# Banks for the last chunk's norm transposes, the first pair's first split, and later splits of the second matrix's tiles, in a fused decoder layer

## The chip, the cores and the metric

The kernel runs on one core of a Trainium2 chip. The metric is the device time of one execution in microseconds (us). The core has five engines that run at the same time, each through its own list of instructions in order: PE (TensorE, matrix products and transposes), DVE (VectorE), ACT (ScalarE), POOL (GpSimd) and SP (SyncE, which here only issues transfers). They wait for each other through semaphores. PE writes its results to PSUM, a small memory of banks; DVE or ACT must read a bank before PE may start something new in it.

## The reference

One layer of a decoder for a prompt of 1024 tokens and 8 sample tokens (1032 tokens together), width 1024, feed-forward width 2816, all in fp32:

```
h = x * (1 + scale1) + shift1
[q,k,v | rq,rk,rv,rg | ga,gb] = h @ w_in
A = dilated sliding-window attention @ w_att_out ;  B = retention @ w_ret_out
x = LN1(alpha * x + gate1 * ((sigmoid(ga) * A + sigmoid(gb) * B) @ w_o))
x = LN2(alpha * x + gate2 * SwiGLU(x * (1 + scale2) + shift2))
```

What follows is about three steps of it: the product with `w_o`, the first layer norm (LN1), and the feed-forward part, whose first matrix `w_ffn_in` holds a gate half g and an up half u, and whose second matrix is `w_ffn_out`.

## The kernel before

**Products.** Every fp32 operand is split into a high and a low part (hi and lo) that PE takes in its fp32r type, and each product is three matmuls: hi by hi, hi by lo, lo by hi. A split is a cast on ACT (hi) and a subtraction on DVE or POOL (lo). Weights come as tiles of 128 x 8 x 128 from the pool `stream` with three buffers each for raw, hi and lo. PSUM banks have four tags: d (three banks), a (two), b (two), o (one). Larger SBUF tiles come from `slots`, a queue of free buffers: whoever takes a buffer that was used before waits for its last readers.

**Order.** Up to the output projection a scheduler of the language may move instructions. From there on `pe`, `dve`, `act`, `pool` and `sp` are wrappers (class `InOrder`, whose call is line 116), which keep the order in which the code is written. That is why most rows below show line 116; they are told apart by the names of their tiles.

**Output projection.** Lines 1168 on run over four chunks of tokens, `for ci in (3, 2, 1, 0)`, and in each over eight weight tiles f = 0 to 7. `wo_cols(f)` issues the load of tile f on SP's queue (line 944) and splits it: even tiles on DVE, odd ones on POOL. PE then makes 24 matmuls into a bank d, and ACT empties the bank into one of four tiles `gm` (line 1180), two weight tiles to each. After every tile `step_pending()` advances the norms of the chunks before by one step.

**Norms.** `norm_chunk` makes two blocks of 128 tokens for a chunk; `norm_block` first transposes the eight parts of `gm` into two banks a, four in each, adds the residual into x on DVE, takes mean and variance (`bn`, `bnmv`), the square root on ACT (`bnr`, line 593) and scales x. Its second half transposes x into two banks b, from which `h2` (the input of the feed-forward part) is scaled and shifted. For the last chunk (ci = 0, the branch `fixed`) the instructions are in written order, and ACT does the scaling and all of `h2`. The blocks of this chunk are stepped within the first pairs of the feed-forward part.

**First matrix in pairs.** A pair i takes 128 columns of g and of u and makes both for half of the tokens in seven products instead of eight, with sums of weights and of tokens (a scheme of Winograd's kind). `pair_load(q)` loads g and u (512 KB each) on SP's queue; `pair_sums(q)` forms four sums of weights on POOL (`w_s`, `w_s4`, and u in place); `pair_split(q, j)` splits the four weight tiles, j = 0 to 3; `combine` sums and splits the tokens into X1 to X7. `pair_steps` holds the products: two accumulations go on in a bank b and a bank a over several products, and each is copied out on ACT or summed on DVE into c11, c12, c21, c22 before the next product is added to it. These names show in the rows as `c`. There are 26 jobs q: 0 to 3 with token half 1 alone, 4 to 21 with both halves, 22 to 25 with half 0 alone. Results go to DRAM as `ffd`.

**Second matrix.** While jobs 22 to 25 run, the results of half 1 come back: `ff_load` brings a tile (`ffr`, 260 KB) on SP's queue and `ff_split` splits it into `xk`, one after each step s_ from job 22 on. `out_load(G)` loads the weights of group G of the second matrix; in job 25 at steps 0, 1 and 2 for groups 0, 1 and 2, and their splits stand at steps 3 and 5 and after the loop. Behind the loop stand the loads and splits of `xk` that are left, and then the groups of products, three to each 128 output columns, whose result rows y pass through LN2.

Of the kernel before, what the change touches and what calls it, by code (L numbers as in the profile page):

```python
# [121 lines left out]
def tile_hybrid_decoder_step(ctx: ExitStack, tc: tile.TileContext, a, o):  # L122
    nc = tc.nc
# [27 lines left out]
    def abank(shape=(128, 512)):  # L151
        return bank("a", shape, 2)

    def bbank(shape=(128, 512)):
        return bank("b", shape, 2)
# [14 lines left out]
    def split(raw, hi, lo, eng=nc.vector):  # L170
        nc.scalar.copy(hi, raw)  # L171
        eng.tensor_sub(lo, raw, hi.bitcast(F32))  # L172
# [108 lines left out]
    pb = bbank((128, 48))  # L281
# [657 lines left out]
        act.copy(hi, raw)  # L939
        dve.tensor_sub(lo, raw, hi.bitcast(F32))  # L940

    def wo_cols(f):
        raw = stream.tile([128, 8, 128], F32, tag="raw", name="w_raw")
        dma_w.dma_start(raw[:], a["w_o"][:, 128 * f:128 * f + 128].rearrange("(k p) c -> p k c", p=128))
        hi = stream.tile([128, 8, 128], F32R, tag="hi", name="w_hi")
        lo = stream.tile([128, 8, 128], F32R, tag="lo", name="w_lo")
        split(raw[:], hi[:], lo[:], nc.gpsimd if f % 2 else nc.vector)
        return hi, lo

    def norm_block(tb, rows, gm, t0, h2):  # L950
        fixed = t0 == 0
        V, A = (dve, act) if fixed else (nc.vector, nc.scalar)
        x = slots.alloc((128, D), name="x1")
        dma_o.dma_start(x[:rows], a["x_prompt"][tb:tb + rows] if tb < S else a["x_sample"])
        for half in range(2):
            pz = abank((rows, 512))
            for j in range(4):
                f = 4 * half + j
                pe.transpose(pz[:, 128 * j:128 * j + 128],
                             gm[f // 2][:, f % 2, tb - t0:tb - t0 + rows], ident[:])  # L960
            c = slice(512 * half, 512 * half + 512)
            V.scalar_tensor_tensor(x[:rows, c], x[:rows, c], ALPHA, pz, op0=OP.mult, op1=OP.add)
        st = late.tile([128, 2, 6], F32, tag="bn", name="bn", bufs=2)
        for i in range(2):
            V.bn_stats(st[:rows, i, :], x[:rows, 512 * i:512 * i + 512])
        mv, r = ln_aggr(st, rows, V, A)
        if fixed:
            nb = late.tile([128, 1], F32, tag="nb", name="nb", bufs=2)
            V.tensor_scalar(nb[:rows], mv[:rows, 0:1], r[:rows], -1.0, op0=OP.mult, op1=OP.mult)
            A.activation(x[:rows], x[:rows], AF.Identity, scale=r[:rows], bias=nb[:rows])  # L970
        else:
            V.tensor_scalar(x[:rows], x[:rows], mv[:rows, 0:1], r[:rows], op0=OP.subtract, op1=OP.mult)
        dma_o.dma_start(xr[tb:tb + rows], x[:rows])
        yield
        for half in range(2):
            pb = bbank((128, 4, rows))
            for j in range(4):
                f = 4 * half + j
                pe.transpose(pb[:, j, :], x[:rows, 128 * f:128 * f + 128], ident[:rows, :rows])
            c4 = slice(4 * half, 4 * half + 4)  # L980
            if tb < S:
                for j in range(4):
                    f = 4 * half + j
                    if half or fixed:
                        A.activation(h2[:, f, :], pb[:, j, :], AF.Identity, bias=B2[:, f, 8:9],
                                             scale=G2[:, f, 8:9])
                    else:
                        V.tensor_scalar(h2[:, f, :], pb[:, j, :], G2[:, f, 8:9], B2[:, f, 8:9],
                                                op0=OP.mult, op1=OP.add)
            else:  # L990
                nc.vector.tensor_mul(h2[:, c4, :], pb, G2[:, c4, 0:NB])
                nc.vector.tensor_add(h2[:, c4, :], h2[:, c4, :], B2[:, c4, 0:NB])
        slots.free(x)
        yield
# [71 lines left out]
    def pair_sums(q):  # L1066
        if q >= NJ:
            return
        g, _, u, _ = raws[q]
        s_, e = slots.alloc((128, 8, 128), name="w_s"), slots.alloc((128, 4, 128), name="w_s4")  # L1070
        pool.tensor_add(s_[:, 4:8, :], u[:, 0:4, :], u[:, 4:8, :])
        pool.tensor_sub(s_[:, 0:4, :], s_[:, 4:8, :], g[:, 0:4, :])
        pool.tensor_sub(e[:], g[:, 4:8, :], s_[:, 0:4, :])
        pool.tensor_sub(u[:, 0:4, :], g[:, 0:4, :], u[:, 0:4, :])
        raws[q] = [g, s_, u, e]

    def pair_split(q, j):
        if q >= NJ:
            return
        raw = raws[q][j]  # L1080
        if j < 3:
            hi, lo = [stream.tile([128, 8, 128], F32R, tag=n, name="w_" + n)[:] for n in ("hi", "lo")]
        else:
            t = slots.alloc((128, 8, 128), F32R, name="w4")
            ring[q] = t
            hi, lo = t[:, 0:4, :], t[:, 4:8, :]
        psplit(raw[:], hi, lo)
        if j:
            slots.free(raw)
        if rolling[0]:  # L1090
            roll(hi)
        ring[q, j] = (hi, lo)
# [74 lines left out]
    for ci in (3, 2, 1, 0):  # L1167
        t0, n = QCH[ci]
        gm = [slots.alloc((128, 2, 264), name="gm") for _ in range(4)]
        for f in range(8):  # L1170
            ps = dbank((128, n))
            o0 = t0 % 512
            whi, wlo = wo_cols(f)
            for k, m in enumerate(mix):
                xhi, xlo = m[ci // 2][:, 0, o0:o0 + n], m[ci // 2][:, 1, o0:o0 + n]
                pe.matmul(ps, whi[:, k, :], xhi, start=k == 0, stop=False)
                pe.matmul(ps, whi[:, k, :], xlo, start=False, stop=False)
                pe.matmul(ps, wlo[:, k, :], xhi, start=False, stop=k == 7)
            dst = gm[f // 2][:, f % 2, :]
            nc.scalar.activation(dst[:, :256], ps[:, :256], AF.Copy, scale=modT[:, GATE1 + f, 8:9])  # L1180
            if n > 256:
                nc.vector.tensor_mul(dst[:, 256:n], ps[:, 256:n], modT[:, GATE1 + f, 0:NB])
            step_pending()
            if ci == 0 and f == 4:
                pair_load(0)
            if ci == 0 and f == 6:
                pair_sums(0)
        if ci % 2 == 0:
            slots.free(*[m[ci // 2] for m in mix])
        pending.append(after_chunk(ci, gm))  # L1190
        if ci == 0:
            pair_load(1)
            pair_split(0, 0)
            pair_split(0, 1)

    xk = [{}, {}]
# [18 lines left out]
    def out_load(G):  # L1215
        if G >= NG:
            return
        _, f, o0, nk = GROUPS[G]
        raw = graw[G] = stream.tile([128, nk, 128], F32, tag="raw", name="w_raw")
        ks = ORDER[o0:o0 + nk]  # L1220
        k1 = next((j for j in range(1, nk) if ks[j] != ks[j - 1] + 1), nk)
        for j0, j1 in ((0, k1), (k1, nk)):
            if j1 > j0:
                sp.dma_start(raw[:, j0:j1, :], w_fo[128 * ks[j0]:128 * (ks[j0] + j1 - j0), 128 * f:128 * f + 128]
                             .rearrange("(k p) c -> p k c", p=128))
# [14 lines left out]
    for q, (i, halves) in enumerate(JOBS):  # L1240
        rolling[0] = len(halves) == 2
        if q == FFC:
            free_x({1: [t for p in X[1].values() for t in p]})
        steps = [pair_steps(q, i, half) for half in halves]
        for s_ in range(7):
            for _ in range(2):
                for g_ in steps:
                    next(g_)
            if s_ == 0:
                pair_split(q, 2)  # L1250
                pair_sums(q + 1)
            elif s_ == 1:
                pair_split(q, 3)
                pair_load(q + 2)
            elif s_ == 2:
                pair_split(q + 1, 0)
            elif s_ == 4:
                pair_split(q + 1, 1)
            if q < LEAD and s_ % 2 == 0:
                step_pending()  # L1260
            if q >= FFC:
                if waiting:
                    ff_split(waiting.popleft())
                for _ in range(1 if len(slots.free_list) >= 6 and kq < FFC else 0):
                    waiting.append(ff_load(1, ORDER[kq]))
                    kq += 1
            if q == NJ - 1:
                if s_ in (0, 1, 2):
                    out_load(s_)
                if s_ in (3, 5):  # L1270
                    out_split(s_ // 2 - 1)
        slots.free(ring[q])
# [204 lines left out]
```

## Time and profile before

| | |
|---|---|
| runs | 1928.22, 1928.94, 1923.56 us; median 1928.22 |
| profiled execution | 1921.71 us, of which the span shown is 1919.9 |
| mean granted clock of PE in it | 0.983 of full speed |
| PE busy | 1826.7 us, 95% of the span |
| weight loads on PE (beside the matmuls) | 1736.6 us, 90% |
| DVE, ACT, POOL busy | 979.9 (51%), 680.9 (35%), 365.0 (19%) |
| moved by DMA | 256.39 MB |

The profiled execution is one run of the kernel with the hardware profiler; all rows come from it. A busy share is a mean over the whole span, so it doesn't tell where an engine waits. The views used below do: busy time by stretch, what an engine waited for in a stretch, the list of one engine's instructions in order of time with the idle time ahead of each and what ended it, and the chain of work followed back from the end. Names are those of the tiles in the code, `out<-in`; a digit behind a name is left out in them, so X1 to X7 are X, h2 is h and c4 is c.

### The profile page before, as it was taken

How to read it: one execution, taken by the hardware profiler on the slowest of the kernel's cores; microseconds unless marked ns; L12 is line 12 of the kernel's file. 1: busy time of each engine (PE TensorE's matmuls, PEld its weight loads, DVE VectorE, ACT ScalarE, POOL GpSimd, SP SyncE). 2: the span in 40 equal slices, each digit the busy share in tenths (PEclk: the TensorE clock that was granted, in tenths of full speed). 3: DMA queues.
4: the chain of work that ended last, by engine and by line, in shares of the span. 5: the costliest groups of instructions: out<-in, count | busy, mean ns of one | idle time of the engine just before them, and what ended most of it. 6: DMA issues, size and time to landing. Idle time of an engine off the chain costs nothing.

```text
span 1919.9 us, 33798 instructions
## 1 busy us (share of the span) xinstructions
PE 1826.7 (95%) x13974; PEld 1736.6 (90%) x13974; DVE 979.9 (51%) x2020; ACT 680.9 (35%) x1338; POOL 365.0 (19%) x435
## 2 busy tenths in 40 slices
PE   7999999999999999999999976999999997999997
PEld 5979889889899998999999965999999997999997
DVE  4733636686534432211555956555455457534844
ACT  3252332443434342122424645333333335223321
POOL 2000010330100000000004345444444343100000
PEclk9999999999999999999999988999999998899999
DMA  9312131681321344431116552356777535525631
GB/s 283 94 37 95 35 104 34 159 289 45 103 67 58 95 151 135 152 112 53 56 53 188 189 175 77 124 162 196 247 241 253 205 91 181 177 88 160 195 120 64
DMA packets 271627, 256.39 MB, mean 134 GB/s; under 512 B 9749, under 2 KB 251261, under 8 KB 270706
## 3 DMA queue, kind: packets, MB, share of 16 engines
q1 hardware_dynamic: 251170, 149.02, 26.8%
q0 software_dynamic: 20176, 105.12, 15.9%
q8 instruction: 109, 1.79, 0.4%
q14 instruction: 44, 0.36, 0.1%
q10 hardware_dynamic: 128, 0.10, 0.0%
HBM read 223.30 MB, written 74.94 MB: 155 GB/s over the span
## 4 chain that ended last, share of the span: by engine, by line
PE 69%; issue 14%; DVE 5%; DMA 5%; POOL 3%; ACT 3%; SPq 1%; DVEq 0%; POOLq 0%; ACTq 0%
PE ps_d L116 10%; PE ps_b L116 10%; PE ps_d L208 9%; PE ps_d L210 9%; PE ps_d L209 9%; PE ps_a L116 5%; PE ps_d L376 2%; PE ps_d L374 2%; PE ps_d L375 2%; POOL w_s L116 2%; PE ps_a L490 1%; PE ps_b L508 1%; PE ps_o L517 1%; DMA vb<-dv 1%; PE ps_a L241 1%
## 5 line engine op out<-in xcount | busy, mean ns | idle before, releaser
L208 PE MATMUL ps_d<-h_hi,w_hi 128*128 128x384 f32 (+1 forms) x1008 | 325.3, 323 | 0.0
L210 PE MATMUL ps_d<-h_hi,w_lo 128*128 128x384 f32 (+1 forms) x1008 | 323.5, 321 | 0.0
L209 PE MATMUL ps_d<-h_lo,w_hi 128*128 128x384 f32 (+1 forms) x1008 | 323.1, 321 | 0.0
L172 DVE TENSOR_TENSOR w_lo<-w_raw,w_hi 128x1024 fp32r<-128x1024 f32 x88 | 103.8, 1179 | 255.3 <-ACT w_hi L171 254.7
L116 PE MATMUL ps_b<-X,w_hi 128*128 128x260 f32 (+1 forms) x1056 | 199.5, 289 | 22.0 <-ACT c L116 20.5
L116 DVE TENSOR_TENSOR w_lo<-w_raw,w_hi 128x1024 fp32r<-128x1024 f32 (+1 forms) x100 | 132.8, 1330 | 163.8 <-ACT w_hi L116 163.7
L171 ACT CAST w_hi<-w_raw 128x1024 fp32r<-128x1024 f32 x104 | 103.9, 999 | 259.2 <-PE ps_d L209 200.1
L208 PEld LDWEIGHTS ps_d<-h_hi,w_hi 128*128 128x128 f32 x1008 | 189.3, 188 | 5.2 <-DVE A L859 3.3
L210 PEld LDWEIGHTS ps_d<-h_hi,w_lo 128*128 128x128 f32 x1008 | 189.5, 188 | 1.7 <-issue 1.2
L209 PEld LDWEIGHTS ps_d<-h_lo,w_hi 128*128 128x128 f32 x1008 | 189.5, 188 | 0.8 <-issue 0.4
L116 PEld LDWEIGHTS ps_b<-X,w_hi 128*128 128x128 f32 x1056 | 167.5, 194 | 23.8 <-ACT c L116 22.1
L116 PE MATMUL ps_b<-X,w_lo 128*128 128x260 f32 (+1 forms) x528 | 152.0, 288 | 0.8 <-DVE w_lo L116 0.8
L116 ACT CAST w_hi<-w_raw 128x1024 fp32r<-128x1024 f32 (+1 forms) x100 | 101.2, 1014 | 107.4 <-PE ps_b L116 91.6
L116 PE MATMUL ps_d<-X,w_hi 128*128 128x260 f32 (+1 forms) x704 | 132.8, 289 | 0.0
L116 PE MATMUL ps_d<-xk,w_hi 128*128 128x260 f32 (+1 forms) x704 | 130.3, 285 | 0.0
L376 PE MATMUL ps_d<-w_lo,h_hi 128*128 128x256 f32 x448 | 127.3, 285 | 0.7 <-DVE w_lo L172 0.7
L116 PE MATMUL ps_b<-xk,w_hi 128*128 128x260 f32 (+1 forms) x704 | 127.7, 282 | 0.0
L374 PE MATMUL ps_d<-w_hi,h_hi 128*128 128x256 f32 x448 | 127.5, 285 | 0.0
L375 PE MATMUL ps_d<-w_hi,h_lo 128*128 128x256 f32 x448 | 126.7, 283 | 0.0
L116 PEld LDWEIGHTS ps_d<-X,w_hi 128*128 128x128 f32 x704 | 112.2, 195 | 0.0
L116 PEld LDWEIGHTS ps_d<-xk,w_hi 128*128 128x128 f32 x704 | 109.6, 191 | 0.1
L116 PEld LDWEIGHTS ps_b<-xk,w_hi 128*128 128x128 f32 x704 | 108.3, 189 | 0.0
(363 smaller groups left out, 4168.9 us busy)
## 6 DMA issues: line engine op xcount, KB each, us to landing
w_raw<-w_in SPq DMA_DIRECT2D x56, 512.0 KB, 4.4
w_raw<-w_ffn_in SPq DMA_DIRECT2D x52, 512.0 KB, 5.0
ada_raw<-w_ada SPq DMA_DIRECT2D x32, 512.0 KB, 4.8
w_raw<-w_o SPq DMA_DIRECT2D x32, 512.0 KB, 4.5
w_raw<-w_ffn_out SPq DMA_DIRECT2D x32, 512.0 KB, 3.7
sample_k<-cache_k POOLq DMA_DIRECT2D x8, 2047.0 KB, 8.8
sample_v<-cache_v POOLq DMA_DIRECT2D x8, 2047.0 KB, 9.4
ada_raw<-w_ada SPq DMA_DIRECT2D x32, 256.0 KB, 5.1
```

The lines of the kernel that those rows point to most:

```text
L116: return self.tc.keep_in_program_order(f(*args, **kw))
L171: nc.scalar.copy(hi, raw)
L172: eng.tensor_sub(lo, raw, hi.bitcast(F32))
L208: nc.tensor.matmul(ps, whi[:, k0 + k, :], xhi[:, t0:t0 + n], start=f, stop=False)
L209: nc.tensor.matmul(ps, whi[:, k0 + k, :], xlo[:, t0:t0 + n], start=False, stop=False)
L210: nc.tensor.matmul(ps, wlo[:, k0 + k, :], xhi[:, t0:t0 + n], start=False, stop=l)
L241: nc.tensor.matmul(ps[32 * g:32 * g + 32], cs[:, k0 + k, :], w[:, k], start=k0 + k < 4, stop=k0 + k >= 4)
L374: nc.tensor.matmul(ps[:, j, :], xh, whi, start=k == 0, stop=False)
L375: nc.tensor.matmul(ps[:, j, :], xl, whi, start=False, stop=False)
L376: nc.tensor.matmul(ps[:, j, :], xh, wlo, start=False, stop=k == 7)
L490: nc.tensor.matmul(sb[hh][:, p, :nk], qT[p][r, 128 * bi:128 * bi + 128], kT[p][r, k0:k0 + nk], start=True, stop=True)
L508: nc.tensor.transpose(pb[:, j, :], pm[h][:, 128 * b:128 * b + 128], ident[:])
```

## The change

It has three parts.

- The norm transposes of the last chunk (`fixed`) no longer go through the banks a and b, which the pairs use for accumulations that stay open over several products. Their first half goes to bank o, the second to a bank d.
- The weights of pair 0 are asked for behind tile 6's load (after f = 5) and no longer behind tile 5's (after f = 4). The sums of pair 0 and the split of its first tile stand ahead of the evacuation of tile 7, and no longer after tile 6 and after the loop. Tile 7 is split on DVE instead of POOL.
- In jobs 22 to 25 `ff_split` is called only while more than two loaded tiles are waiting, so splits come later, and more of them are left for after the loop. The weights of groups 0 and 1 of the second matrix are asked for in job 24, at steps 3 and 5, and those of group 2 in job 25 at step 2.

```
-    def wo_cols(f):
+    def wo_cols(f, eng):
...
-        split(raw[:], hi[:], lo[:], nc.gpsimd if f % 2 else nc.vector)
+        split(raw[:], hi[:], lo[:], eng)
...
-            pz = abank((rows, 512))
+            pz = (abank if not fixed else dbank if half else obank)((rows, 512))
...
-            pb = bbank((128, 4, rows))
+            pb = (bbank if not fixed else dbank if half else obank)((128, 4, rows))
...
-            whi, wlo = wo_cols(f)
+            whi, wlo = wo_cols(f, nc.gpsimd if f % 2 and (ci or f < 7) else nc.vector)
...
+            if ci == 0 and f == 7:
+                pair_sums(0)
+                pair_split(0, 0)
             nc.scalar.activation(dst[:, :256], ps[:, :256], AF.Copy, scale=modT[:, GATE1 + f, 8:9])
...
             step_pending()
-            if ci == 0 and f == 4:
+            if ci == 0 and f == 5:
                 pair_load(0)
-            if ci == 0 and f == 6:
-                pair_sums(0)
...
         if ci == 0:
             pair_load(1)
-            pair_split(0, 0)
             pair_split(0, 1)
...
             if q >= FFC:
-                if waiting:
+                if len(waiting) > 2:
                     ff_split(waiting.popleft())
...
+            if q == NJ - 2 and s_ in (3, 5):
+                out_load(s_ // 2 - 1)
             if q == NJ - 1:
-                if s_ in (0, 1, 2):
-                    out_load(s_)
+                if s_ == 2:
+                    out_load(2)
```

How this moves instructions shows best in the lists of the built kernels. SP's queue around the loads of pair 0 (`w_ffn_in`; `w_o` are the tiles of the output projection, the last three of 32 being tiles 5, 6 and 7 of the last chunk), before:

```order
L944 DMA w_raw<-w_o 128x8x128 x29
L116 DMA w_raw<-w_ffn_in 128x8x128
L116 DMA w_raw_328_11522<-w_ffn_in 128x8x128
L944 DMA w_raw<-w_o 128x8x128 x3
L116 DMA w_raw<-w_ffn_in 128x8x128
L116 DMA w_raw_331_11628<-w_ffn_in 128x8x128
```

and after:

```order
L944 DMA w_raw<-w_o 128x8x128 x30
L116 DMA w_raw<-w_ffn_in 128x8x128
L116 DMA w_raw_328_11554<-w_ffn_in 128x8x128
L944 DMA w_raw<-w_o 128x8x128 x2
L116 DMA w_raw<-w_ffn_in 128x8x128
L116 DMA w_raw_331_11632<-w_ffn_in 128x8x128
```

Tile 5's load has passed the two loads of pair 0, which stand ahead of tile 6's now.

ACT at the end of the output projection (`gm_11273` takes tiles 4 and 5, `gm_11274` tiles 6 and 7; the casts of line 116 are the pair's), before:

```order
L171 CAST w_hi<-w_raw 128x1024
L985 ACTIVATE h_326_11364<-ps_b,B_10198,G_10197 128x128 x4
L171 CAST w_hi<-w_raw 128x1024
L1180 ACTIVATE gm_11273<-ps_d,modT 128x256 x2
L1180 ACTIVATE gm_11274<-ps_d,modT 128x256 x2
L116 CAST w_hi<-w_raw 128x1024
L116 CAST w_hi<-w_s_11589 128x1024
L116 COPY c_332_11639<-ps_b 128x260
```

and after, where the evacuation's line is 1183:

```order
L171 CAST w_hi<-w_raw 128x1024
L985 ACTIVATE h_326_11364<-ps_b,B_10198,G_10197 128x128 x4
L171 CAST w_hi<-w_raw 128x1024
L1183 ACTIVATE gm_11273<-ps_d,modT 128x256
L116 CAST w_hi<-w_raw 128x1024
L1183 ACTIVATE gm_11273<-ps_d,modT 128x256
L1183 ACTIVATE gm_11274<-ps_d,modT 128x256 x2
L116 CAST w_hi<-w_s_11620 128x1024
L116 COPY c_332_11639<-ps_b 128x260
```

The first cast of pair 0 has moved ahead of the evacuations of tiles 5, 6 and 7; the cast of its sum `w_s` has stayed behind them.

PE where the first block of the last chunk is transposed, between the first and the second product of pair 0, before:

```order
L116 MATMUL ps_b<-X_306_11107,w_lo 128x260
L116 MATMUL ps_a<-ident,gm_11271 128x128 x2
L116 MATMUL ps_a<-ident,gm_11272 128x128 x2
L116 MATMUL ps_a<-ident,gm_11273 128x128 x2
L116 MATMUL ps_a<-ident,gm_11274 128x128 x2
L116 MATMUL ps_d<-X_308_11109,w_hi 128x260
```

and after:

```order
L116 MATMUL ps_b<-X_306_11107,w_lo 128x260
L116 MATMUL ps_o<-ident,gm_11271 128x128 x2
L116 MATMUL ps_o<-ident,gm_11272 128x128 x2
L116 MATMUL ps_d<-ident,gm_11273 128x128 x2
L116 MATMUL ps_d<-ident,gm_11274 128x128 x2
L116 MATMUL ps_d<-X_308_11109,w_hi 128x260
```

The place among PE's instructions is the same; the banks differ.

DVE in job 22 (`xk` are the splits of the second matrix's tiles, `w_lo` and `w_483` those of the pair's weights, `c` its sums), before:

```order
L116 TENSOR_TENSOR c_478_16521<-c_478_16521,ps_d 128x256
L116 TENSOR_TENSOR w_483_16564<-w_s_475_16329,w_483_16564 128x512
L116 TENSOR_TENSOR xk_16548<-ffr_16546,xk_16548 128x520
L116 TENSOR_TENSOR w_lo<-w_raw,w_hi 128x1024
L116 TENSOR_TENSOR xk_16575<-ffr_16573,xk_16575 128x520
L116 TENSOR_TENSOR xk_16597<-ffr_16595,xk_16597 128x520
L116 TENSOR_TENSOR c_478_16521<-c_478_16521,ps_a 128x256
```

and after:

```order
L116 TENSOR_TENSOR c_478_16521<-c_478_16521,ps_d 128x256
L116 TENSOR_TENSOR w_483_16564<-w_s_475_16329,w_483_16564 128x512
L116 TENSOR_TENSOR w_lo<-w_raw,w_hi 128x1024
L116 TENSOR_TENSOR xk_16548<-ffr_16546,xk_16548 128x520
L116 TENSOR_TENSOR c_478_16521<-c_478_16521,ps_a 128x256
```

Three splits of `xk` stood ahead of the sum with bank a (c22); one is left there. Of the 22 tiles of half 1, 15 instead of 19 are split within jobs 22 to 25, and seven instead of three behind the loop.

## Rows read from the trace of the kernel before

**Rows 1.** Busy time by stretch: length, PE, PEld, DVE, ACT, POOL, PEclk, DMA share, GB/s.
```profile
1100.00:1150.00 50.00, 36.32 (x275) 35.49 (x275) 26.48 (x41) 22.55 (x37) 23.41 (x17) 0.90 0.59 180
1150.00:1200.00 50.00, 31.50 (x207) 30.61 (x207) 33.39 (x40) 26.45 (x51) 25.71 (x19) 0.81 0.24 74
1600.00:1650.00 50.00, 41.70 (x297) 41.09 (x298) 31.75 (x44) 22.80 (x40) 13.09 (x16) 0.86 0.55 160
```

**Rows 2.** PE's waits, 1020 to 1220: waited for, us in total, times, longest.
```profile
PE ps_b L116 <- ACT h L116: 10.6, 2, 8.2
PE ps_b L116 <- ACT c L116: 8.6, 3, 4.8
PE ps_a L116 <- DVE x L116: 6.8, 1, 6.8
PE ps_b L116 <- DVE x L972: 4.6, 1, 4.6
...
PE ps_b L116 <- ACT w_hi L116: 1.5, 1, 1.5
...
PE ps_b L116 <- DVE w_lo L116: 0.8, 1, 0.8
```

**Rows 3.** PE's waits, 1500 to 1700.
```profile
PE ps_b L116 <- ACT c L116: 11.8, 5, 3.9
PE ps_d L116 <- DVE w_lo L116: 4.5, 1, 4.5
PE ps_a L116 <- DVE c L116: 2.3, 1, 2.3
```

**Rows 4.** The chain that ended last, 1095 to 1215: start, us, what.
```profile
1108.07 6.03 DMA w_raw<-w_o
...
1197.64 2.97 PE ps_b L116 x12
...
1202.27 1.45 PE ps_a L116 x12
```

**Rows 5.** SP's queue near 1103: start, us, line, operation, out<-in.
```profile
1103.65 0.99 SPq L116 DMA_DIRECT2D w_raw<-w_ffn_in  x2
```

**Rows 6.** ACT in order of time: start, us, operation, idle time before and what ended it.
```profile
1114.20 1.04 ACT L171 CAST w_hi<-w_raw 128x1024 fp32r<-128x1024 f32 x1 [6.30 <-DMA w_raw<-w_o]
1115.15 0.29 ACT L593 ACTIVATE bnr<-bnmv,eps 128x1 f32<-128x1 f32 x1
...
1132.87 1.04 ACT L116 CAST w_hi<-w_raw 128x1024 fp32r<-128x1024 f32 x1
...
1154.43 0.38 ACT L116 COPY c<-ps_b 128x260 f32<-128x260 f32 x1 [0.69 <-PE ps_b L116]
...
1168.48 1.50 ACT L116 ACTIVATE h<-ps_b,B,G 128x128 f32<-128x128 f32 x4 [1.21 <-PE ps_b L116]
1171.24 0.42 ACT L116 ACTIVATE c<-c 128x260 f32<-128x260 f32 x1 [1.26 <-DVE c L116]
...
1175.68 1.51 ACT L116 ACTIVATE h<-ps_b,B,G 128x128 f32<-128x128 f32 x4 [0.75 <-PE ps_b L116]
1178.59 0.38 ACT L116 COPY c<-ps_b 128x260 f32<-128x260 f32 x1 [1.40 <-PE ps_b L116]
```

**Rows 7.** DVE in order of time, three places.
```profile
1112.04 0.19 DVE L917 BATCH_NORM_AGGREGATE bnmv<-bn 128x2 f32<-128x12 f32 x1
...
1133.93 1.23 DVE L116 TENSOR_TENSOR w_lo<-w_raw,w_hi 128x1024 fp32r<-128x1024 f32 x1 [12.10 <-ACT w_hi L116]
...
1653.55 1.23 DVE L116 SCALAR_TENSOR_TENSOR y<-y,ln_g 128x1024 f32<-128x1024 f32 x1 [9.53 <-DMA y<-xr]
```

**Rows 8.** All writers of tile xk: count, ns least/median/most, first to last start.
```profile
L116 ACT CAST xk<-ffr x44: 608/622/632, 1582.5 to 1784.0; 128x520 fp32r<-128x520 f32 x22, 128x512 fp32r<-128x512 f32 x22
L116 DVE TENSOR_TENSOR xk<-ffr,xk x44: 685/693/1799, 1584.2 to 1784.6; 128x520 fp32r<-128x520 f32 x22, 128x512 fp32r<-128x512 f32 x22
```

**Rows 9.** ACT in the last pair.
```profile
1630.49 0.62 ACT L116 CAST w<-w_s 128x512 fp32r<-128x512 f32 x1 [2.54 <-DMA ffd<-c]
```

## The prediction: what the change will do to the time

> **What bounds the kernel now.** I read the page first: TensorE (PE) is busy for 95% of the span, and after its start the slices fall below 9 tenths in two places only. The view of busy time by stretch says the same with numbers: 36.32 and 31.50 us busy of 50 between 1100 and 1200, with the granted clock down to 0.90 and 0.81 of full speed (the mean of a level of 2.4 and one of 1.2 GHz), and 41.70 of 50 at 0.86 after 1600 [rows 1]. Everywhere else a change of an idle engine is worth nothing. So the second view is that of PE's waits in these two stretches: 32.9 us in six rows of the first, 18.6 in three of the second [rows 2, 3]. The first stretch is the passage from the output projection (`w_o`, chunk 0, eight weight tiles f = 0 to 7) to the first feed-forward pairs; there the norms of chunks 1 and 0 are still under way. The second is the last four pairs, in which ScalarE (ACT) and VectorE (DVE) also split the tiles of the second matrix. The diff touches just these two.
>
> **Step A, the pair's weights asked for one tile later.** SyncE's queue issues tile 5's load behind the two loads of pair 0: the pair at 1103.65, tile 5 at 1108.07, landing 6.03 us later [rows 4, 5]. ACT's cast of tile 5 therefore starts at 1114.20, after 6.30 us of idle time, and behind it in ACT's queue stands the square root of a norm, at 1115.15 [rows 6]. Its input, the variance, was ready at 1112.04 + 0.19 [rows 7]; from it comes the row x for which PE waits 4.6 us [rows 2]. The change puts tile 5 into the place of 1103.65, 4.42 us earlier, so the cast starts no later than 1109.8 on the same landing, or when its buffer comes free just after, and the square root then waits for the variance alone: 1115.15 - 1112.3 = **2.85 us** off PE's wait. The next one late is the same row x, with 1.75 us left. Pair 0's own weights are now asked for at 1108.07. With 6.03 us each and even one behind the other they land by 1120.2, and their first cast runs at 1132.87 now [rows 6], about 1123 then: hidden, with 3 us in hand. Without that cover each late microsecond would count, since four evacuations stand behind the cast.
>
> **Step B, the first half of pair 0 split before the last evacuations.** In ACT's order the cast moves ahead of the evacuations of tiles 5 to 7, so it and its DVE half no longer run after PE's last `w_o` product. PE's waits for w_hi (1.5) and w_lo (0.8) go: **2.3 us** [rows 2]. The cast itself (1.04) stands in front of tile 5's evacuation, which only matters when a third accumulator bank is wanted, two products later: nothing. The sums of pair 0 on GpSimd (POOL) stay behind tile 5's split in its queue as before, and lose tile 7's split, which goes to DVE; DVE has 12.10 us idle there [rows 7], so 1.2 us more cost nothing. The added wait is the cast's, on tile 5's product (its buffer) and on the load; queued behind it are the evacuations of tiles 5 to 7 and the cast of w_s, and PE waits for these.
>
> **Step C, the norm transposes in banks o and d.** The row to avoid is the simplest sum. PE's waits for x in ps_a (6.8) and for h in ps_b (8.2 and 2.4, together 10.6) go away by name, 17.4 us [rows 2]. But ACT and DVE work through a fixed queue here (copies, casts, norms, table loads), and PE's products only have to be ready when that queue asks. What the banks are worth is the time in which ACT itself waited for PE, while PE waited for ACT to empty a bank. In ACT's queue that is 0.69 before the copy at 1154.43, 1.21 before h at 1168.48, 1.26 at 1171.24 (DVE's sum, which waited for PE), 0.75 at 1175.68 and 1.40 at 1178.59 [rows 6]: **5.3 us**. The other 12 us come back as waits for the copies c (8.6 now), since a product that continues an accumulation needs its bank copied first. After the change PE reaches each such product early and waits there for its copy instead, some 3 us at a time. A new one could be bank o: there is one, and block 1's transposes need DVE to have read block 0's; DVE does that right behind two splits, about when PE gets there: 0 to 0.6, and not on ACT's path.
>
> GpSimd's sums of pair 1 (four operations) lay beside an idle DVE and would now overlap the end of DVE's first splits. A tile split takes 0.69 alone and up to 1.80 beside GpSimd [rows 8]: 0 to 1.1 us; I take 0, since the sums end before the split that the norm stands behind. The Trainium skill ("SBUF — State Buffer", the section on shared port pairs) has it as an exclusive lock, the later instruction blocked until the first ends, for VectorE operations with two SBUF inputs. By that one GpSimd operation at most would be waited out, and the sum would be about a microsecond smaller; the 1.80 of the row is the nearest sight of it.
>
> **The clock.** After the waits products run at the lower level: 12 matmuls take 2.97 us at 1197.64 and 1.45 at 1202.27 [rows 4]. In 1100 to 1150 that costs 36.32 x 0.10 = 3.6 us [rows 1]. Shorter waits may give back 0 to 3.6 of it; I take 1.5, since the 4.6 us wait is the only one before the queue of step C takes over.
>
> **Step D, the second matrix.** Two of the three splits that stood ahead of the first pair's sum c22 move behind it; at 0.69 to 1.80 each [rows 8] that is 1.4 to 3.6 us on DVE, of which PE's wait for c (2.3) can give back no more than itself [rows 3]. With the one cast (0.62) that leaves ACT's queue ahead of a copy, I take 2.1, and 0.5 for the cast that leaves the third pair's. In the last pair ACT waits 2.54 for a store of c [rows 9], whose landing competes with the loads of the output weights; two of these are now asked for earlier: 0 to 2.5, taken 1.2. Against that, seven tiles instead of three are split after the loop. Four splits more (2.8 on DVE) lie in the 9.53 us that DVE spends idle before the rows y arrive [rows 7]; without this cover they would count in full. Two loads of 260 KB more go out there, ahead of the store and the loads of y, on which the wait of 4.5 for w_lo hangs [rows 3]: 0 to 6.0 (a 512 KB load's whole time, [rows 4]), taken 1.0, since most of a landing is overlapped. Together **2.8 us**, between -2 and 5.8.
>
> **Sum.** 2.85 + 2.3 + 5.3 + 1.5 + 2.8 = 14.75 us. The profiled execution took 1921.71, which would become 1907.0. It lies 6.5 below the median of the three runs (1928.22); on that median the forecast is 1913.5. With every term at its lower end (1.5, since tile 5 may still land a little late; 1.5, the w_hi wait alone; half of C; no clock; -2) the gain is 3.6 us, 1924.6; at the upper ends 19.9, 1908.3. Differences of 0.3% (5.8 us) are about what a measurement here tells from none.
>
> **Rivals.**
> 1. *The banks only rename the waits.* ACT's four waits of step C come back as waits for the single bank o or for a bank d that DVE has not emptied. Then C is worth the 0.69 and D nothing: 2.85 + 2.3 + 0.7 = 5.9, 1922.3. For it: PE in order, one bank o. Against it: bank d's readers (the sum c11, the second half of x) run several microseconds before their next writer.
> 2. *The tail gives it back.* The first stretch gains 12, but the seven late splits and five late loads push the rows y and the fourth group's w_lo back by up to 6.0: 1928.2 - 12 + 6.0 = 1922.2 at worst, 1919 in the middle. For it: the DMA queue is the releaser there already. Against: 9.53 us of slack on DVE.
> 3. *Slower: the clock in the last four pairs.* Many waits of 2 to 4 us evenly spread could hold PE at the lower level. 28 products then cost 28 x (2.97 - 1.45) = 42.6 more, less the waits they would swallow (11.8 + 2.3) and the 41.70 x 0.14 = 5.8 already lost: +22.7. With D's gain lost, 1928.2 - 12 + 22.7 = 1938.9. It decides from about half the products on. Against it: with the same kind of waits the rows show 0.86. The Trainium skill ("TensorE: Matmul & The Clock Gate", the section on psum-queue depth-cycling) tells of such a kernel, whose PE idles a little between groups in cycling PSUM banks and goes back and forth between the levels. By that the products would be split between 1.45 and 2.97; the trace agrees that both occur, and its share of the lower level is the smaller one.
>
> **How the numbers follow.** Forecast 0.60; rival 1 0.17; rival 2 0.15; rival 3 0.04; something unseen that leaves no change 0.04. The range reaches from the upper ends and the runs' own spread (1908.3 - 4) to rivals 1 and 2: 1904 to 1923. Faster by over 0.3%: 0.60 + 0.07 + 0.13 = 0.80; within: 0.10 + 0.02 + 0.03 = 0.15; slower: 0.05.
>
> **What would show it.** In PE's waits of the first stretch: those for x in ps_a, for h, w_hi and w_lo gone; that for L972 down to about 1.8; those for copies c up from 8.6 to some 12, with a few for DVE's c. ACT's cast of tile 5 near 1110; PE's first pair product near 1129, ahead of the time at which its weight is cast now (1132.87); the copy that now ends PE's wait of 4.8 at 1189, near 1177. In the second: the wait for DVE's c under 1, that for w_lo still 4 to 6. If the casts of pair 0 idle on a load, or h is still waited for, A or C is wrong; if PE's waits shrink by 17 and the span by 5, C's reading of ACT's queue is too generous.

## The result

| | before | changed |
|---|---|---|
| median of all runs | 1925.89 us (4 runs, 1921.79 to 1928.94) | 1905.23 us (4 runs, 1903.49 to 1910.46) |
| span of the profiled execution | 1919.9 us | 1902.2 us |
| mean granted clock of it | 0.983 | 0.987 |
| PE, DVE, ACT, POOL busy | 95, 51, 35, 19% | 96, 52, 36, 19% |

The ratio is 0.9899, with a 95% interval of 0.9869 to 0.9928: the change makes the kernel about 1.0% faster, 19 us on 1925.89. The forecast was 1913.5 and faster, in a range of 1904 to 1923.

The view of busy time by stretch of the changed kernel, for the stretches of [rows 1] (the third begins 18 us earlier, since the same work does; columns as there):

```profile
1100.00:1150.00 50.00, 41.80 (x326) 41.01 (x326) 33.31 (x49) 26.72 (x44) 22.66 (x17) 0.92 0.63 190
1150.00:1200.00 50.00, 37.96 (x254) 36.54 (x254) 38.35 (x42) 27.40 (x56) 33.26 (x23) 0.84 0.27 80
1582.00:1632.00 50.00, 42.42 (x318) 41.80 (x318) 36.36 (x49) 26.10 (x45) 17.97 (x19) 0.90 0.62 180
```

PE is busy for 5.5 and 6.5 us more of the first two, and the granted clock is a little higher in all three. PE's waits in the first passage, which answer to [rows 2], and in the second, to [rows 3]:

```profile
PE ps_b L116 <- ACT c L116: 15.2, 5, 5.1
PE ps_a L116 <- DVE c L116: 3.7, 3, 2.3
PE ps_b L116 <- ACT h L985: 3.2, 1, 3.2
PE ps_o L116 <- DVE x L116: 1.3, 1, 1.3
PE ps_a L116 <- ACT gm L1183: 0.6, 1, 0.6
PE ps_b L116 <- ACT gm L1183: 0.5, 1, 0.5
PE ps_o L116 <- ACT h L116: 0.4, 1, 0.4
...
PE ps_b L116 <- ACT c L116: 8.5, 5, 3.8
PE ps_d L116 <- DVE w_lo L116: 5.3, 1, 5.3
PE ps_a L116 <- DVE c L116: 1.6, 1, 1.6
```

All the waits that the forecast called gone are gone by name: for x in ps_a (6.8), for h in ps_b (10.6), for w_hi and w_lo of pair 0 (2.3). The one for x of line 972 (4.6), of which it left 1.75, is gone too. Two sizes were missed: the waits for the copies c grew from 8.6 to 15.2 (some 12 forecast), as 17.4 us of waits by name became some 5 us of time, and in the second passage the wait for DVE's c is 1.6 (under 1 forecast). ACT's row shows why. Where it stood idle for PE in [rows 6], there is no idle time now:

```profile
1147.30 0.35 ACT L116 COPY c<-ps_b 128x260 f32<-128x260 f32 x1
...
1158.66 1.50 ACT L116 ACTIVATE h<-ps_o,B,G 128x128 f32<-128x128 f32 x4
1160.04 1.52 ACT L116 ACTIVATE h<-ps_d,B,G 128x128 f32<-128x128 f32 x4
1161.41 0.46 ACT L116 ACTIVATE c<-c 128x260 f32<-128x260 f32 x1
...
1166.20 0.47 ACT L116 COPY c<-ps_b 128x260 f32<-128x260 f32 x1
```

### Where the time went: leads at fixed places

One number for each stage is had by matching instructions. ACT makes the same 132 copies c from ps_b and the same 32 evacuations z of the second matrix in every kernel here, in the same order. The **lead** is the time of one of them in the trace of before less its time in the other trace. The start is an evacuation of chunk 1 (1075.72 before), ahead of all that is changed; the others stood at 1137.06, 1178.59, 1570.83, 1634.92, 1652.82 and 1907.53 before. In us:

| kernel | start | copy 1 | copy 6 | copy 120 | copy 132 | first z | last z |
|---|---|---|---|---|---|---|---|
| changed | 0.5 | 8.1 | 12.4 | 12.4 | 18.1 | 19.6 | 17.7 |
| changed, second execution (e14) | -0.1 | 6.6 | 11.8 | 11.0 | 16.7 | 18.1 | 19.8 |
| changed, rows y later (e9) | 0.4 | 7.0 | 11.3 | 11.3 | 16.9 | 18.3 | 26.3 |
| changed, sums of pair 1 later (e10) | 0.6 | 7.1 | 11.6 | 10.3 | 15.7 | 17.1 | 16.6 |
| changed, x back in banks a (e7) | -3.6 | 4.2 | 7.4 | 6.6 | 12.3 | 13.7 | 14.2 |
| pair 0 alone (e2) | 1.4 | 8.0 | 5.1 | 5.2 | 4.5 | 4.5 | 5.0 |
| banks alone (e1) | -0.8 | 1.5 | 7.5 | 6.5 | 7.0 | 7.6 | 7.3 |
| pair 0's load alone (e4) | -3.8 | -1.2 | -1.2 | -1.2 | -1.7 | -1.5 | -2.4 |
| second matrix alone (e3) | 1.5 | 1.7 | 1.4 | 1.5 | 7.4 | 8.8 | 8.4 |
| splits later alone (e5) | 0.8 | 4.0 | 3.4 | 3.5 | 5.5 | 6.0 | 6.4 |
| loads earlier alone (e6) | 0.7 | -1.0 | -2.4 | -2.2 | 1.1 | 2.5 | 3.8 |

Between copy 6 and copy 120, some 390 us, no lead moves by more than 1.3. So the change acts in two passages, and each can be read by itself: steps A and B up to copy 1, step C from there to copy 6, step D behind copy 120. The forecast put 11.95 on A, B, C and the clock, and 2.8 on D. The profiled pair shows 11.9 from the start (12.4 - 0.5) and 5.3 (17.7 - 12.4). The starts (-3.8 to 1.5) and the leads of e3, e5 and e6 at copy 6 (-2.4 to 3.4, with all ahead of it unchanged) say how far single executions differ, so a stage is read as the difference of two columns (0.1 of it can be rounding).

### The profile page after: what moved, and what is told of

Its sections match the earlier page's. It is cut to its first block, busy times and chain, and to the rows that moved or that the text cites. A ratio compares the mean times of both kernels' runs of the same rounds, so it can differ in the third digit from the quotient of the medians.

```text
span 1902.2 us, 33801 instructions
## 1 busy us (share of the span) xinstructions
PE 1822.9 (96%) x13974; PEld 1732.9 (91%) x13974; DVE 984.1 (52%) x2021; ACT 679.7 (36%) x1338; POOL 365.5 (19%) x434
## 4 chain that ended last, share of the span: by engine, by line
PE 74%; issue 12%; DVE 5%; DMA 4%; ACT 3%; POOL 2%; SPq 1%; DVEq 0%; POOLq 0%; ACTq 0%
PE ps_d L116 12%; PE ps_b L116 11%; PE ps_d L208 9%; PE ps_d L210 9%; PE ps_d L209 9%; PE ps_a L116 6%; PE ps_d L376 2%; PE ps_d L374 2%; PE ps_d L375 2%; PE ps_a L490 1%; PE ps_b L508 1%; PE ps_o L517 1%; PE ps_a L241 1%; DVE y L116 1%; DMA qb<-dq 1%
```

## The experiments

### The three parts, each alone

**e1**: the two lines of `norm_block` that choose the banks.

```
-            pz = abank((rows, 512))
+            pz = (abank if not fixed else dbank if half else obank)((rows, 512))
...
-            pb = bbank((128, 4, rows))
+            pb = (bbank if not fixed else dbank if half else obank)((128, 4, rows))
```

> The kernel before with only the banks of the last chunk's norm transposes changed (o and d in place of a and b). Theory (what counts is the time ACT itself waited for PE): PE's waits for x in ps_a and for h go, waits for the copies c grow, and the span shortens by 4.3 to 5.3 us; the second stretch stays as before. Rival (the waits are only renamed, one bank o): under 1 us. A naive reading of PE's waits by name: 17.4 us.

Measured: 1915.41 us (median), ratio 0.9971 (0.9956 to 0.9986), that is 5.6 us. (The kernel before has a median of 1923.62 beside e1 to e4. The ratio on record is not that of the two medians, which differ by 8.2 here, and the interval goes with it; so the gains of e1 to e4 are told by the ratio.) The lead grows by 6.0 between copies 1 and 6, in three jumps: 0.8 at copy 3, 2.9 at copy 5, 2.4 at copy 6. ACT's idle times in [rows 6] before these three places are 0.69, then 1.21 + 1.26 = 2.47, then 0.75 + 1.40 = 2.15. The waits for x in ps_a and for h are gone from PE's list, those for the copies c stand at 15.8. The theory held place by place, with a sum a little above its 4.3 to 5.3; neither "renamed" nor "by name" did.

**e2**: pair 0's load after f = 5, its sums and first split at f = 7, tile 7 split on DVE; banks as before.

> The kernel before with only the part on pair 0: its load after f = 5, its sums and first split ahead of the last evacuation, tile 7's split on DVE; the banks as before. Theory (the parts add): the first copy c leads the one of before by 8 to 9 us, and since ACT's fixed queue starts that much earlier, 7 to 8.5 us remain at the end of pair 2. Rival (the banks are what lets it through): PE's waits for x and h grow by what was gained, and under 3 us remain.

Measured: 1918.29 us, ratio 0.9975 (0.9959 to 0.9992), that is 4.8 us. The first copy leads by 8.0, as in the changed kernel, but only 5.1 are left at copy 6. That lies between the theory and the rival: PE's wait for x grew by 2.6, that for h not at all:

```profile
PE ps_b L116 <- ACT h L116: 10.6, 2, 8.2
PE ps_a L116 <- DVE x L116: 9.4, 2, 8.1
...
PE ps_d L116 <- DVE w_lo L172: 2.0, 2, 1.9
```

In the leads the parts therefore don't simply add: the banks were worth 6.0 alone, and 4.3 + 2.9 = 7.2 when pair 0 is early. The times are too coarse to show this: by the ratios e1, e2 and e3 gain 5.6 + 4.8 + 9.2 = 19.6 us, and the changed kernel 19.

**e3**: only the second matrix's edits (`if len(waiting) > 2`, and the three calls of `out_load` earlier).

> The kernel before with only the second matrix's part: splits later, and the loads of the output weights earlier. Theory from the trace of after: 6 to 7 us are gained up to the first product of the second matrix, of which ACT's wait for the store of c (2.54) and the clock behind it are the larger part, and about 2 are given back where the half changes, so 4 to 6 us in the span. Rival (the forecast's sum): 2.8 us. Rival (the gain hung on the first stretch being shorter): under 1.

Measured: 1913.29 us, ratio 0.9952 (0.9931 to 0.9973), that is 9.2 us, above the 4 to 6 that were expected. From copy 120 to the first z the lead grows by 7.3, with the first passage unchanged; to the last z by 6.9. So this part has the whole gain of the second passage by itself and needs nothing of the first, and the "given back where the half changes" that the changed kernel's trace showed (from 20.0 to 17.7) is not in it.

**e4**: only the load of pair 0.

```
-            if ci == 0 and f == 4:
+            if ci == 0 and f == 5:
                 pair_load(0)
```

> The kernel before with only pair 0's load asked for after f = 5 in place of f = 4. Theory: ACT's cast of tile 5 no longer waits for a load, PE's wait for x of line 972 falls from 4.6 to between 0.5 and 1.8, and 3 to 4 us are left in the span. Rival (tile 7's split on GpSimd, behind the sums, is late): 0 to 2 us, with a wait of PE for w_lo before the last tile. Rival (pair 0's weights land too late): slower.

Measured: 1922.39 us, ratio 0.9987 (0.9969 to 1.0005): 2.5 us, which can't be told from no change; 3 to 4 were expected. The wait for x of line 972 (4.6) is gone from PE's list, as expected, but from the start to copy 1 the lead grows by 2.6 only (this execution had lost 3.8 ahead of the start, where nothing is changed). After the same wait of 3.2 us for h of line 985 the granted clock from 1050 to 1100 was 0.93 here, and 1.00 in the trace of before; and the waits for pair 0's first weights stayed, 3.1 for 2.3:

```profile
PE ps_b L116 <- DVE w_lo L116: 1.6, 1, 1.6
PE ps_b L116 <- ACT w_hi L116: 1.5, 1, 1.5
```

### What of the second matrix's part it is

> The kernel before with only the splits of the second matrix's tiles made later; the loads of the output weights as before. Theory A (the splits' room on DVE is the small part, the store of c the large one): about 1.2 to 1.7 us of lead by the end of job 23, and ACT's wait of 2.54 for the store of c in the last pair stays, so 1 to 2 us in all up to the first product of the second matrix. Theory B (the splits are what freed the last pair): 5 us or more there, and the wait for the store is gone.

**e5** (only `if len(waiting) > 2`): 1915.52 us beside 1920.98, one run each. Up to copy 128 the lead grows from 3.5 to 5.3, and ACT's wait in the last pair is still there:

```profile
1625.65 0.62 ACT L116 CAST w<-w_s 128x512 fp32r<-128x512 f32 x1 [2.98 <-DMA ffd<-c]
```

> The kernel before with only the loads of the output weights asked for earlier; the splits as before. Theory A: nothing gained up to job 24, then ACT's wait of 2.54 for the store of c is gone, PE's wait of 3.86 in the last pair falls by 2.5 to 3, its products behind it run at the higher clock, and 4 to 5.5 us are gained at the first product of the second matrix. Theory B: under 1 us, the store's wait stays.

**e6** (only the calls of `out_load`): 1917.90 beside 1920.98. From copy 120 to copy 130 nothing is gained (-2.2, then -2.8); then the wait for the store is gone, and by the first z the lead has grown by 4.7 from copy 120:

```profile
1630.67 0.60 ACT L116 CAST w<-w_s 128x512 fp32r<-128x512 f32 x1
```

Theory A held in both, though e5's 2.5 to the first z is above its 1 to 2. The two shares, 2.5 and 4.7, come to the 7.3 of e3, in part by chance: e5's PE waits 4.39 in the last pair, more than before, and about 1.1 of its 2.5 is that the 36 products behind this wait took 5.86 and not 6.99.

### What the banks of x and of h are worth

> The changed kernel with the x transposes of the last chunk put back into the banks a; the h transposes stay in o and d. Theory (a bank is worth the time that ACT itself waited for PE: 0.7 of the 5.3): PE waits 6.5 to 8 us for x in ps_a again, and yet the lead of the first stretch falls by 0.7 to 1.6 us only. Rival (PE's waits count by name): it falls by 5 us or more.

**e7** (the changed kernel with `pz = abank((rows, 512))`): 1907.86 beside 1920.98, one run each. PE waits longer for x in ps_a than the 6.5 to 8 expected, and the lead from copy 1 to copy 6 is 3.2 in place of 4.3 to 5.2.

```profile
PE ps_a L116 <- DVE x L116: 9.4, 2, 8.1
```

So 9.4 us of a wait by name cost 1.1 to 2.0. The place says it closer: from copy 3 to copy 6 the six traces with h in the banks o and d (e1, e7, e9, e10, e14 and the changed kernel's first) all gain 5.2 to 5.3, and from copy 2 to copy 3 e7 loses 0.3 where e1, e9, e14 and the changed kernel gain 0.8. So the banks of x are worth 1.1. The rival that counts waits by name is out.

### GpSimd's sums beside DVE's splits

> The changed kernel with GpSimd's four sums of pair 1 put behind block 0's norm in its queue. Theory (the sums slow DVE's splits ahead of the first norm, 2.18 and 2.30 us in place of 1.22 and 1.23, and this costs the path 1.8 us): both splits take 1.2 to 1.3, the lead at the second copy c is 1.5 to 2 us larger than in the changed kernel, of which 0.5 to 2 remain at the end of pair 2, since the sums now lie beside block 1's splits. Rival (the splits are hidden by ACT's queue): no change of that lead, or a loss as w_s comes late.

**e10** moves one call behind a `step_pending()`:

```
             if s_ == 0:
                 pair_split(q, 2)
-                pair_sums(q + 1)
+                if q:
+                    pair_sums(q + 1)
...
             if q < LEAD and s_ % 2 == 0:
                 step_pending()
+                if q == s_ == 0:
+                    pair_sums(1)
```

DVE in order of time, first of the changed kernel, then of e10, where the same two splits stand ahead of the sum that the norm needs:

```profile
1128.91 2.18 DVE L116 TENSOR_TENSOR w_lo<-w_s,w_hi 128x1024 fp32r<-128x1024 f32 x1 [4.83 <-PE ps_b L116]
1131.01 2.30 DVE L116 TENSOR_TENSOR w_lo<-w_raw,w_hi 128x1024 fp32r<-128x1024 f32 x1
1133.24 0.67 DVE L116 SCALAR_TENSOR_TENSOR x<-x,ps_o 128x512 f32<-128x512 f32 x1
```
```profile
1129.98 1.23 DVE L116 TENSOR_TENSOR w_lo<-w_s,w_hi 128x1024 fp32r<-128x1024 f32 x1 [4.94 <-PE ps_b L116]
1131.34 1.23 DVE L116 TENSOR_TENSOR w_lo<-w_raw,w_hi 128x1024 fp32r<-128x1024 f32 x1
1132.48 0.68 DVE L116 SCALAR_TENSOR_TENSOR x<-x,ps_o 128x512 f32<-128x512 f32 x1
```

The lead from copy 1 to copy 2 falls by 1.8 in the changed kernel and not at all in e10: the slowing is on the path. But the sums now lie beside block 1's splits:

```profile
1139.52 1.76 DVE L116 TENSOR_TENSOR w<-w_s,w 128x512 fp32r<-128x512 f32 x1 [3.21 <-ACT w L116]
1141.20 2.30 DVE L116 TENSOR_TENSOR w_lo<-w_raw,w_hi 128x1024 fp32r<-128x1024 f32 x1
```

From copy 2 to copy 3 the lead of e10 falls by 0.7, where that of the changed kernel and of e1 grows by 0.8, so it pays 1.5 there; at copy 6 it is 4.5 above copy 1 (changed: 4.3). The theory's first half held, its hope that 0.5 to 2 remain did not: the price is paid once, ahead of one norm or the other. 1905.43 beside 1920.98.

### The wait that is left, and a second trace

> The changed kernel with the first residual step of the second matrix's part (four sums of rows y on DVE) left out in group 0 and so begun in group 1, behind the split of group 3's weights instead of ahead of it. Theory (PE's wait of 5.3 for w_lo is DVE's queue, in which the split stands behind rows that wait for a transfer; the weight itself is cast 6 us before): the wait goes, the products behind it start at the higher clock, and the span is 5 to 6.3 us shorter than that of the changed kernel. Rival (group 3's weights themselves are late): the wait stays, no change. Rival (what is gained is given back where the half changes, by loads of the other half's tiles): 2 to 4 us.

**e9** is the changed kernel with one condition more:

```
-        if todo and o0 < 16:
+        if todo and o0 < 16 and G:
             residual(todo.popleft())
```

DVE in the changed kernel first: the split for which PE waits 5.3 us stands behind four sums of y, and these behind a transfer.

```profile
1634.85 1.23 DVE L116 SCALAR_TENSOR_TENSOR y<-y,ln_g 128x1024 f32<-128x1024 f32 x1 [6.79 <-DMA y<-xr]
1636.11 1.22 DVE L116 SCALAR_TENSOR_TENSOR y<-ln_b,y 128x1024 f32<-128x1024 f32 x1
1637.25 1.22 DVE L116 SCALAR_TENSOR_TENSOR y<-y,ln_g 128x1024 f32<-128x1024 f32 x1
1638.50 1.23 DVE L116 SCALAR_TENSOR_TENSOR y<-ln_b,y 128x1024 f32<-128x1024 f32 x1
1639.64 1.22 DVE L116 TENSOR_TENSOR w_lo<-w_raw,w_hi 128x1024 fp32r<-128x1024 f32 x1
```

Then in e9, where PE's list for 1500 to 1700 has no wait for w_lo any more:

```profile
1630.85 1.23 DVE L116 TENSOR_TENSOR w_lo<-w_raw,w_hi 128x1024 fp32r<-128x1024 f32 x1 [1.59 <-ACT w_hi L116]
1635.53 1.23 DVE L116 SCALAR_TENSOR_TENSOR y<-y,ln_g 128x1024 f32<-128x1024 f32 x1 [3.46 <-DMA y<-xr]
```

Measured: 1896.64 us (1895.89 to 1899.42), ratio to before 0.9865 (0.983 to 0.9901); beside it on the same chip the changed kernel had 1904.43 and 0.9901 (0.9871 to 0.9932). The span is 6.5 below the second trace of the changed kernel. This version is the fastest of those run.

> The changed kernel once more, for a second trace of it and for times on the chip of the run beside it. Theory: the wait of ACT's z at the change of the halves (1.6 us for PE) was this one execution's transfers and is absent or differs; the lead of the first stretch is 12 to 13.6 us, depending on whether the clock falls behind the wait of 3.2 us ahead of it.

**e14**: the changed kernel again, 1904.43 us. The give-back at the change of halves is not there: the lead goes on to 19.8. The first passage's 11.8, which is 11.9 from the start, lies just under the 12 that was expected. In this trace the load of tile 6 is the next one late, with a wait of PE of 1.7 for w_lo of line 172, as in e2 (1.9).

## Why the prediction held, and where its sum was off

**Step A.** The order of events was right: the cast of tile 5 no longer waits for its load, and PE's wait for x of line 972 is gone in every trace with the part on pair 0. Its size was read from one execution. With the order of before, that wait was 4.6, 3.9, 1.5, 5.4 and 0.7 us (before, e3, e5, e6, e1), with 1.00 granted from 1050 to 1100 where it was 3.9 or more, and 0.93 to 0.97 where it was 1.5 or less: a PE that is slower ahead of it comes later to the same load, so the two may partly make up for each other (no run sets the clock by itself). The forecast said that 1.75 would be left; in the changed kernel 0.5 is, and for another thing, the evacuation of a tile. So 4.1 us of wait went where 2.85 were taken. One reason is that the variance was ready earlier too (1111.41 in place of 1112.23), as a DVE operation ahead of it took 0.81 and not 1.78 beside GpSimd's split.

**Step B.** The waits of 2.3 are gone. A and B and the clock up to copy 1, from the start: 6.5 to 7.8 in the six traces with both, -1.7 to 3.2 (mean 0.8) in the five without either (before itself, with 0, and e1, e3, e5, e6). The part of A alone (e4) has 2.6, within the spread of those five, so A's share is read from the waits and not from a time. The difference of the means, 7.0 - 0.8 = 6.2, stands against 2.85 + 2.3 + 1.5 = 6.65. The clock's 1.5 was about right: the 96 products of tiles 4 to 7 behind the former wait took 11.7 in place of 13.0.

**Step C.** This was the choice on which most hung, 5.3 by ACT's own idle time against 17.4 by name, and e1 and e7 bear it out. Alone it measured 6.0, in the changed kernel 4.3. The difference is the term that was set at nothing: GpSimd's sums beside DVE's splits, 0 to 1.1 with 0 taken, cost 1.8 from copy 1 to copy 2 (2.18 + 2.30 in place of 1.23 each). The reason given, that the sums end before the split that the norm stands behind, failed: they start only at 1127.35, when pair 1's weights have landed, while the splits came 6 to 8 us earlier. The Trainium skill ("SBUF — State Buffer", the section "Who interferes with whom"), which has the port pair that the two engines share as an exclusive lock, was named for this with one GpSimd operation waited out. The trace agrees with the lock and not with the "one", which was the forecast's own: each split waits out one, 0.95 + 1.07 us. GpSimd waits too: its sum that starts beside the first split takes 2.15 where the one ahead of it takes 1.28.

```profile
1128.73 1.28 POOL L116 TENSOR_TENSOR w_s<-w_s,w_raw 128x512 f32<-128x512 f32 x1
1130.08 2.15 POOL L116 TENSOR_TENSOR w_s<-w_raw,w_s 128x512 f32<-128x512 f32 x1
```

The second trace of the changed kernel (e14) is a test that nobody planned. There the first split starts 0.04 us ahead of a sum and takes its usual time, the sum is the one that waits, and only the second split is slowed:

```profile
1130.44 1.23 DVE L116 TENSOR_TENSOR w_lo<-w_s,w_hi 128x1024 fp32r<-128x1024 f32 x1 [5.00 <-PE ps_b L116]
1131.79 2.10 DVE L116 TENSOR_TENSOR w_lo<-w_raw,w_hi 128x1024 fp32r<-128x1024 f32 x1
...
1130.48 2.33 POOL L116 TENSOR_TENSOR w_s<-w_s,w_raw 128x512 f32<-128x512 f32 x1
```

The lead there falls by 0.9 from copy 1 to copy 2, and from copy 1 to copy 6 it grows by 5.2. With this price added back the banks are worth 4.3 + 1.8 in the changed kernel, 5.2 + 0.9 in e14 and 4.3 + 1.8 in e9, within 0.1 of e1's 6.0 each time.

**Step D.** This term was mis-sized: 2.8, from -2 to 5.8, where the lead grows from copy 120 to the first z by 6.8 to 7.3 in the six traces that have the whole part, 7.2 in the changed kernel's. Its pieces in the changed kernel: 1.7 up to copy 128 (splits; forecast 2.1 + 0.5), 2.7 where ACT waited for the store (taken 1.2, with 2.5 as its end), and 2.66 of clock, which the sum left out. The last 36 products of the pairs, before and after: PE's wait ahead of the first of them, then their view by stretch (columns as in [rows 1]):

```profile
1631.95 0.79 PE L116 MATMUL ps_b<-X,w_hi 128*128 128x256 f32 x2 [3.86 <-ACT c L116]
...
1631.95:1638.94 6.99, 6.99 (x36) 6.99 (x37) 3.57 (x6) 2.21 (x3) 1.05 (x2) 0.58 0.51 154
```
```profile
1615.09 0.50 PE L116 MATMUL ps_b<-X,w_hi 128*128 128x256 f32 x2 [1.15 <-ACT c L116]
...
1615.09:1619.42 4.33, 4.33 (x36) 4.33 (x37) 3.26 (x6) 2.22 (x3) 1.06 (x2) 1.00 0.83 253
```

A wait of 3.86 ahead of them became one of 1.15, and with it the granted clock was 1.00, the level of 2.4 GHz throughout, and not 0.58, which lies near the lower one. The size differs by execution: in the five traces in which this wait stands (3.86 to 4.44 us: before, e1, e2, e4, e5) the 36 products took 5.86 to 6.99, in the seven in which it is 1.15 to 1.52 they took 4.33 to 4.38. So the term is 1.5 to 2.7. The first passage's sum had such a clock term and D's had none, though [rows 4] gave the price. Against that the forecast took 1.0 for the tail: the wait for w_lo went from 4.5 to 5.3 in one trace and to 4.2 in the other, so about nothing.

**Rivals.** Rival 1 (bank o renames the waits) is out: 1.3 + 0.4 us of waits on ps_o. Rival 2 (the tail gives it back) was seen in one trace, 2.3 of 20.0 where the halves change, and to that size in no other; in ACT's queue the evacuation z stands there behind casts of xk, which wait for transfers (8.1 us in nine pieces between 1740 and 1765). Why these were slower in that execution is open. Rival 3 (the lower clock in the last pairs) went the other way: from 0.86 to 0.90 over them, and to 1.00 in the last three products.

So the first passage came out at 11.9 from the start (forecast 11.95). The mechanism was right, but that the sum agrees so closely is luck: A's wait gave 1.25 more than was taken, and C 1.0 less. The second passage came out at 5.3 to 8.8 (forecast 2.8). The time, 1905.2, lies 8.3 below the forecast, near the lower end of its range. Of this 2.3 are the base, since the forecast started from a median of 1928.22 over three runs and a fourth run made it 1925.89; the other 5.9 have the size of what D exceeded its term by (2.5 to 6.0).

## What to carry to other kernels

A bank that is freed was worth, in this kernel, the time for which the engine with the fixed queue stood idle for it, not the time for which the other engine is said to wait; read the idle time in the queue that sets the pace. A wait of some 4 us on PE cost itself and a lower clock behind it (1.5 to 2.7 us on 36 products here), so where it is removed both belong into the sum, the second as a range. A wait that ends with a transfer should be priced from more than one execution, and work that doesn't need it should stand ahead of it in an in-order queue: e9's span is 6.5 us shorter for that.

## What the runs showed of the hardware

- After one and the same wait of PE of 3.2 us (for h of line 985) the granted clock over 1050 to 1100 was 1.00 in five traces (before, e2, e3, e6, e14) and 0.93 to 0.97 in seven (the changed kernel's first, e1, e4, e5, e7, e9 and e10). From that wait to the next transposes into banks a PE took 15.7 us in the one case (before) and 18.0 in the other (e1): 2.3 us from one execution to the next, with no edit near.
- In the changed kernel's first trace DVE's split of 128x1024 took 1.23 us alone and 2.18 and 2.30 beside GpSimd's sums, and GpSimd's sum 1.28 alone and 2.15 and 2.26 beside it: the two take turns. In e14 the split that started 0.04 us ahead of a sum took 1.23, and the sum 2.33: there the one that started first paid nothing.
- Behind a PE wait of 3.86 to 4.44 us the same 36 products took 5.86 to 6.99 us, behind one of 1.15 to 1.52 they took 4.33 to 4.38.
